# UP with 512 moving columns, the routing's second parts on GpSimd, 16-bit index lookups, and norms spread a unit later in a two-block transformer kernel

## The chip, the cores and the metric

One core of a Trainium2 chip. The metric is the device time of one execution in microseconds (us). Engines: PE (TensorE, matmuls), DVE (VectorE), ACT (ScalarE), POOL (GpSimd), SP (which issues the DMAs of the weights).

## The reference

Two transformer blocks on 256 tokens of 1024 channels in float32, one after the other. The first has an mLSTM beside sliding-window attention, then cross attention to a memory of 256 tokens, then a PEER feed-forward layer. The second has gated linear attention (GLA) beside block attention, an MLP of 4096 and a gated embedding. Each sublayer is led by an RMS norm. The change is in the PEER layer (and in how norms and weights are scheduled):

```python
def peer_ffn(xn, w_pq, sub_keys1, sub_keys2, expert_down, expert_up):   # T = 128 tokens a block
    def block(xb):
        qh = (xb @ w_pq).reshape(T, P_HEADS, 2, P_KEY_DIM)              # 8 heads, 2 halves
        s1 = einsum('thd,nd->thn', qh[:, :, 0], sub_keys1)              # 128 keys each
        s2 = einsum('thd,nd->thn', qh[:, :, 1], sub_keys2)
        v1, i1 = top_k(s1, 16)
        v2, i2 = top_k(s2, 16)
        cand_s = (v1[..., :, None] + v2[..., None, :]).reshape(T, P_HEADS, 256)
        cand_i = (i1[..., :, None] * 128 + i2[..., None, :]).reshape(T, P_HEADS, 256)
        top_s, pos = top_k(cand_s, 16)
        eidx = take_along_axis(cand_i, pos, axis=-1)                    # the lookup
        g = softmax(top_s, axis=-1)
        a = gelu(einsum('thkd,td->thk', expert_down[eidx], xb))
        return einsum('thk,thkd->td', g * a, expert_up[eidx])
```

## The kernel before

*Residual and weights.* The residual `hT` stands with channels in partitions (8 tiles of 128 x 256 tokens). All weights come as one stream of chunks of 128 x 1024 f32 (512 KB), in the order of `ORDER`. `Stream` (from L88) has SP load a chunk into `raw` (4 buffers). `cut_upto` splits it into two parts that the matmuls take: `hi`, a rounded copy (L122, always by ACT here), and `lo` = raw - hi (L123, the second part, by DVE or by GpSimd). Which engine does it stands in `PLAN`: a chunk's name starts a pattern that holds until the next name, and a pattern's letters are A, V, G for ACT, DVE and GpSimd (`AV`: hi on ACT, lo on DVE; from pq2 on GpSimd has two chunks of three, from down52 none, in UP every other one). There are 3 buffers of hi and lo; a chunk is cut when the one two before it is taken. The activations are split too (`XH`, `XL`), and each product is three matmuls: hi by XH, hi by XL, lo by XH.

*Two forms of a product.* `unit_T` (L323 to L325) has the weights as the stationary operand and 256 tokens moving; a chunk is 24 matmuls and gives one tile of 128 outputs. `unit_N` (L362 to L364) has 128 tokens of the activation stationary and 512 columns of weights moving; a chunk is 12 matmuls.

*Order.* All engines' instructions are in the order in which the Python code issues them. `Chains` holds generators, the work beside the stream: after each unit `tick` lets each go on by one step; `yield n` passes n units, to which the table `PAUSES` adds.

*PEER.* After the queries (16 units `pq`) and their scores come 128 units `down`, in which every expert is multiplied with every token (`ev_down`, gelu on ACT). Beside the first 52 units runs `routing()`, on DVE but for the softmax's exp. For each of two blocks of 128 tokens (tb) it does 16 searches of the 16 best of 128 (`top16`, two per unit), 8 searches in 256 candidate sums (L872 builds the sums; one per unit), the softmax (L876 to L880), and two lookups. A lookup turns a candidate's position into the index of a key: L895 compares the position with 0 to 15 (2048 f32 per partition), L898 multiplies by the indices, L899 sums over the 16, and a transpose (L902) brings the result into `eT`. Then `gating()` builds coefficients of all 128 x 128 experts by matmuls of 16-bit one-hot rows (L918 to L922, L941). `UP` follows: for each of 128 chunks, `coef` (L974 by ACT, L975 by DVE) splits a coefficient tile into the `ring`, and `up` (L987 to L989) adds 24 matmuls to four PSUM banks: weights stationary, 256 tokens moving. So UP's sums have channels in partitions, like hT. The last two chunks are taken together; for each pair of output tiles the sums are added to hT (L1013), then scaled and split into XH (L1018) and XL (L1021), while PE multiplies the next pair. At 1121.5 us the second block begins with `bk` (unit_N).

*Norms.* A `norm_chain` (L308) sums squares over channels with a matmul, takes an inverse square root by Newton steps on DVE, makes a diagonal, and `gap` units later `spread` (L305) brings it to all partitions with two matmuls. The cross attention's query norm, FFN's norm and the MLP's and last norms use it; the second block's first norm is written out in `norms` and `along`; the GLA's gate (L1127, L1129) is a chain too.

## Time and profile before

| what | value |
|---|---|
| median of 3 runs | 1644.19 us (1643.83 to 1645.55) |
| the profiled execution | 1648.56 us |
| its span, first to last instruction | 1646.8 us |
| mean granted clock of PE | 0.981 |
| PE / DVE / ACT / POOL busy | 1572.9 / 1207.7 / 798.9 / 392.0 us |
| DMA | 265.52 MB, mean 161 GB/s |

Stages in the profiled execution: the queries' units from 240, the scores from 293, DOWN 301.1 to 752.6 with the routing until 504.9, UP 752.7 to 1121.5, the second block from there. The profile's page gives busy time per engine, then the costliest groups of instructions; other views of the trace show a stretch, an engine's waits with what released them, or single instructions in time. A matmul's duration there is that of its way through the array; how fast PE goes shows in the distance between the starts of two.

### The profile page before, as it was taken

Reading aid. Unit: us, or ns where it says so; the run is one execution under the profiler, and the core shown is the slowest. Engines: PE = TensorE matmul, PEld = TensorE weight load, DVE = VectorE, ACT = ScalarE, POOL = GpSimd, SP = SyncE. Lnnn points to the kernel's source line nnn. Section 1 sums busy time; section 2 is a strip of 40 time slices with the busy share of each in tenths; the row PEclk is TensorE's granted clock in tenths of the full one; section 3 lists DMA queues with packets and bytes.
Section 4 is the critical chain, followed back from the end, with each engine's and each line's share of the span. In section 5 each row is a group of like instructions: output and inputs, shape, how many; then the busy total and the mean of one; then the engine's idle time right before and its main releaser. Section 6 shows DMA issues by size and latency. Waiting matters only on the chain.

```text
span 1646.8 us, 30594 instructions
## 1 busy us (share of the span) xinstructions
PE 1572.9 (96%) x12338; PEld 1515.7 (92%) x12338; DVE 1207.7 (73%) x2073; ACT 798.9 (49%) x1336; POOL 392.0 (24%) x223
## 2 busy tenths in 40 slices
PE   9889989989879999999999999999899999899998
PEld 8788989988879999999999999998698899899998
DVE  6967653788978899976666666668885566777556
ACT  7555443543334555544444444445464643444444
POOL 3210004435530000003444444421030100087000
PEclk9999999999989999999999999999999999999999
DMA  7334444334334444445665555665445345455653
GB/s 263 103 103 156 139 145 154 131 131 162 128 123 158 156 154 154 154 168 178 183 185 184 180 180 184 186 186 166 152 143 164 119 163 179 159 175 190 201 180 128
DMA packets 75726, 265.52 MB, mean 161 GB/s; under 512 B 8368, under 2 KB 11952, under 8 KB 75584
## 3 DMA queue, kind: packets, MB, share of 16 engines
q1 hardware_dynamic: 74848, 262.31, 48.7%
q8 instruction: 96, 1.57, 0.4%
q10 hardware_dynamic: 736, 1.27, 0.2%
q14 instruction: 46, 0.38, 0.1%
HBM read 262.49 MB, written 1.05 MB: 160 GB/s over the span
## 4 chain that ended last, share of the span: by engine, by line
PE 63%; DVE 6%; ACT 1%; issue 1%; POOL 0%; DVEq 0%; POOLq 0%; ACTq 0%
PE mm L323 11%; PE mm L325 11%; PE mm L324 10%; PE at L987 6%; PE at L988 6%; PE at L989 6%; DVE lo L123 2%; PE mm L989 2%; PE mm L988 2%; PE mm L987 2%; PE at L941 2%; PE mm L363 2%; PE mm L362 2%; PE mm L364 2%; ACT hi L122 1%
## 5 line engine op out<-in xcount | busy, mean ns | idle before, releaser
L122 ACT CAST hi<-raw 128x1024 fp32r<-128x1024 f32 (+1 forms) x495 | 515.6, 1044 | 301.0 <-issue 104.9
L123 DVE TENSOR_TENSOR lo<-raw,hi 128x1024 fp32r<-128x1024 f32 (+1 forms) x376 | 469.9, 1252 | 167.1 <-ACT hi L122 164.0
L123 POOL TENSOR_TENSOR lo<-raw,hi 128x1024 fp32r<-128x1024 f32 x119 | 296.2, 2489 | 843.5 <-ACT hi L122 708.4
L325 PE MATMUL mm<-XH,lo 128*128 128x256 f32 x1608 | 464.3, 289 | 32.2 <-DVE lo L123 31.5
L323 PE MATMUL mm<-XH,hi 128*128 128x256 f32 x1608 | 470.9, 293 | 4.8 <-DVE hT L378 4.3
L324 PE MATMUL mm<-XL,hi 128*128 128x256 f32 x1608 | 461.7, 287 | 0.0
L325 PEld LDWEIGHTS mm<-XH,lo 128*128 128x128 f32 x1608 | 315.6, 196 | 35.9 <-DVE lo L123 34.8
L323 PEld LDWEIGHTS mm<-XH,hi 128*128 128x128 f32 x1608 | 315.9, 196 | 6.6 <-issue 5.1
L324 PEld LDWEIGHTS mm<-XL,hi 128*128 128x128 f32 x1608 | 315.9, 196 | 0.2
L975 DVE SCALAR_TENSOR_TENSOR ring<-cb,ring 128x256 fp32r<-128x256 f32 x128 | 173.0, 1353 | 94.1 <-ACT ring L974 94.1
L987 PE MATMUL at<-ring,hi 128*128 128x256 f32 x768 | 217.4, 283 | 1.0 <-DVE cb L961 1.0
L988 PE MATMUL at<-ring,hi 128*128 128x256 f32 x768 | 217.4, 283 | 0.0
L989 PE MATMUL at<-ring,lo 128*128 128x256 f32 x768 | 217.4, 283 | 0.0
L987 PEld LDWEIGHTS at<-ring,hi 128*128 128x128 f32 x768 | 147.4, 192 | 1.2 <-ACT ring L974 1.2
L988 PEld LDWEIGHTS at<-ring,hi 128*128 128x128 f32 x768 | 147.4, 192 | 0.1
L989 PEld LDWEIGHTS at<-ring,lo 128*128 128x128 f32 x768 | 147.5, 192 | 0.0
L958 ACT ACTIVATE cb<-mm 128x256 f32<-128x256 f32 (+32 forms) x117 | 38.2, 326 | 171.7 <-PE mm L325 171.7
L363 PE MATMUL mm<-lo,XH 128*128 128x512 f32 (+1 forms) x208 | 82.0, 394 | 4.8 <-DVE lo L123 4.7
L362 PE MATMUL mm<-hi,XH 128*128 128x512 f32 (+1 forms) x208 | 84.1, 404 | 1.0 <-ACT kn L1336 1.0
L364 PE MATMUL mm<-hi,XL 128*128 128x512 f32 (+1 forms) x208 | 81.6, 392 | 0.8 <-DVE XL L411 0.8
L325 PE MATMUL mm<-MH,lo 128*128 128x256 f32 x256 | 72.5, 283 | 2.0 <-POOL lo L123 1.2
L988 PE MATMUL mm<-ring,hi 128*128 128x256 f32 x256 | 72.5, 283 | 0.0
(460 smaller groups left out, 2932.0 us busy)
## 6 DMA issues: line engine op xcount, KB each, us to landing
raw<-in_wst SPq DMA_DIRECT2D x237, 512.0 KB, 3.3
raw<-in_dwn SPq DMA_DIRECT2D x128, 512.0 KB, 3.3
raw<-in_upw SPq DMA_DIRECT2D x128, 512.0 KB, 4.1
hT<-in_xT SPq DMA_DIRECT2D x4, 256.0 KB, 5.4
memt<-in_memT SPq DMA_DIRECT2D x1, 1024.0 KB, 6.0
out<-hT SPq DMA_DIRECT2D x7, 128.0 KB, 1.7
rowt<-in_rows ACTq DMA_DIRECT2D x1, 640.0 KB, 6.0
raw<-in_wst SPq DMA_DIRECT2D x2, 256.0 KB, 3.9
```

Of the source, the lines that this page charges most:

```text
L122: self.nc.scalar.copy(hi[:, o], raw[:, o])
L123: (self.nc.vector if second == "V" else self.nc.gpsimd).tensor_tensor(lo[:, o], raw[:, o], hi[:, o], op=OP.subtract)
L323: T.matmul(ps, lhsT=wh, rhs=xh, start=start, stop=False)
L324: T.matmul(ps, lhsT=wh, rhs=xl, start=False, stop=False)
L325: T.matmul(ps, lhsT=wl, rhs=xh, start=False, stop=stop)
L362: T.matmul(pss[tb], lhsT=xh, rhs=h, start=kd == 0, stop=False)
L363: T.matmul(pss[tb], lhsT=xh, rhs=l, start=False, stop=False)
L364: T.matmul(pss[tb], lhsT=xl, rhs=h, start=False, stop=kd == 7)
L975: V.scalar_tensor_tensor(lo, cb[:, j], 1.0 / GATE, hi, op0=OP.mult, op1=OP.subtract)
L987: T.matmul(o, lhsT=wh, rhs=ch, start=j == 0 and n % 2 == 0, stop=False)
L988: T.matmul(o, lhsT=wh, rhs=cl, start=False, stop=False)
L989: T.matmul(o, lhsT=wl, rhs=ch, start=False, stop=j == 127 and n % 2 == 1)
```

## The change

Four parts. **UP** becomes the other form: 128 tokens of the coefficients are stationary, 512 columns of weights move, half as many matmuls (12 per chunk). Its sums now have tokens in partitions, so at the end they are copied out of PSUM (one half per token block by ACT, one by DVE, L1041 and L1042), turned by 16 transposes (L1026), added to hT (L1030) and split (L1032, L1034); the second half of the channels follows as a chain after `bk0`. **PLAN**: from xo2 on, GpSimd makes all second parts, but those of down20 to down27 and from down45 on, which are DVE's. **The lookup** works on 16-bit numbers: the indices are copied twice side by side (L896), compare (L898) and product (L902) run over 2048 float16, the sum over 16 is three halving additions (L904) and a last one (L905); a chain step more lies between a lookup and its transpose. **Norms**: the spread comes a unit later (but for the first norm), and so do the second block's first norm and a step of the GLA's gate.

```diff
-          ("along", 1): 2, ("stream", 0): 1, ...
+          ("along", 1): 3, ("stream", 0): 1, ...
-          ("gla", 8): 1, ("gla_out", 2): 1}
+          ("gla", 1): 1, ("gla", 8): 1, ("gla_out", 2): 1}
-PLAN = {"mv0": ("AV",), "pq2": ("AG", "AG", "AV"), "down52": ("AV",), "upw0": ("AV", "AG"), "upw122": ("AV",),
-        "up3": ("AV", "AG"), "up31": ("AV",)}
+PLAN = {"mv0": ("AV",), "xo2": ("AG",), "down20": ("AV",), "down28": ("AG",), "down45": ("AV",),
+        "upw0": ("AV", "AG"), "upw122": ("AV",), "up3": ("AV", "AG"), "up31": ("AV",)}
...
-    def norm_chain(pool, tag, work, nat, dst, total=None, gap=1):
+    def norm_chain(pool, tag, work, nat, dst, total=None, gap=2):
...
-            yield from norm_chain(psA, "at", wk, rx, Rb)
+            yield from norm_chain(psA, "at", wk, rx, Rb, gap=1)
...
-            yield from norm_chain(psA, "at", wk, rm, Rm, total=accm, gap=2)
+            yield from norm_chain(psA, "at", wk, rm, Rm, total=accm, gap=3)
...
-                V.tensor_copy(fi, iu)
...
-                    V.tensor_tensor(cand.rearrange("p h a b -> p (h a) b"),
-                                    pf[:, :, None].to_broadcast([128, 128, 16]),
-                                    iota[:, None, 0:16].to_broadcast([128, 128, 16]), op=OP.is_equal)
-                    V.tensor_tensor(cand, cand, ff[:, :, half, None, :].to_broadcast([128, 8, 16, 16]), op=OP.mult)
-                    V.tensor_reduce(ee, cand.rearrange("p h a b -> p (h a) b"), axis=AX.X, op=OP.add)
-                    yield 4
+                    V.tensor_copy(two, uu[:, :, half].rearrange("p h k -> p k h")[:, :, :, None].to_broadcast(
+                        [128, 16, 8, 2]))
+                    V.tensor_tensor(hit.rearrange("p k (c s) -> p k c s", s=2),
+                                    pf.rearrange("p (c s) -> p c s", s=2)[:, None].to_broadcast([128, 16, 64, 2]),
+                                    iota2[:, 0:16, None, :].to_broadcast([128, 16, 64, 2]), op=OP.is_equal)
+                    h5 = hit.rearrange("p k (h c s) -> p k h c s", h=8, s=2)
+                    V.tensor_tensor(h5, h5, two[:, :, :, None, :].to_broadcast([128, 16, 8, 8, 2]), op=OP.mult)
+                    for n in (8, 4, 2):
+                        V.tensor_tensor(hit[:, 0:n], hit[:, 0:n], hit[:, n:2 * n], op=OP.add)
+                    V.tensor_tensor(ee, hit[:, 0], hit[:, 1], op=OP.add)
+                    yield 5
...
-        sums = [bank(psB, "at") for i in range(3)] + [bank(psB, "mm")]
+        sums = [[bank(psB, "mm") for tb in range(2)] for g in range(2)]
+        nat2 = flat[:, 4096:6144].rearrange("p (a d) -> p a d", a=2)
...
-        def up(j, w, n):
-            o = sums[n // 2][:, (n % 2) * 256:(n % 2) * 256 + 256]
-            wh, wl = (x[:, n * 128:n * 128 + 128] for x in w)
-            ch, cl = coefs[j]
-            T.matmul(o, lhsT=wh, rhs=ch, start=j == 0 and n % 2 == 0, stop=False)
-            T.matmul(o, lhsT=wh, rhs=cl, start=False, stop=False)
-            T.matmul(o, lhsT=wl, rhs=ch, start=False, stop=j == 127 and n % 2 == 1)
+        def up(j, w, tb, g):
+            ch, cl = (c[:, tb * 128:tb * 128 + 128] for c in coefs[j])
+            wh, wl = (x[:, g * 512:g * 512 + 512] for x in w)
+            o = sums[g][tb]
+            T.matmul(o, lhsT=ch, rhs=wh, start=j == 0, stop=False)
+            T.matmul(o, lhsT=ch, rhs=wl, start=False, stop=False)
+            T.matmul(o, lhsT=cl, rhs=wh, start=False, stop=j == 127)
...
-        for i in range(4):
-            for n in (2 * i, 2 * i + 1):
-                for j in range(2):
-                    up(126 + j, last[j], n)
-            k2 = slice(2 * i, 2 * i + 2)
-            V.tensor_tensor(hT[:, k2], sums[i].rearrange("p (a t) -> p a t", a=2), hT[:, k2], op=OP.add)
...
+        def half(g):
+            turned = {}
+            for i in (2 * g, 2 * g + 1):
+                turned[i] = bank(psB, "at")
+                for k in range(2):
+                    for tb in range(2):
+                        o = (2 * i + k) * 128
+                        T.transpose(turned[i][:, k * 256 + tb * 128:k * 256 + tb * 128 + 128], nat2[:, tb, o:o + 128],
+                                    ident)
+            for i in (2 * g, 2 * g + 1):
+                k2 = slice(2 * i, 2 * i + 2)
+                V.tensor_tensor(hT[:, k2], turned[i].rearrange("p (a t) -> p a t", a=2), hT[:, k2], op=OP.add)
+                for n in (2 * i, 2 * i + 1):
+                    A.activation(XH[:, n], hT[:, n], AF.Copy, scale=gfm[:, n:n + 1])
+                for n in (2 * i, 2 * i + 1):
+                    V.scalar_tensor_tensor(XL[:, n], hT[:, n], gfm[:, n:n + 1], XH[:, n], op0=OP.mult,
+                                           op1=OP.subtract)
+
+        for g in range(2):
+            for tb in range(2):
+                for j in range(2):
+                    up(126 + j, last[j], tb, g)
+            A.copy(nat2[:, 0, g * 512:g * 512 + 512], sums[g][0])
+            V.tensor_copy(nat2[:, 1, g * 512:g * 512 + 512], sums[g][1])
+        half(0)
+        ws.cut_upto(ws.taken + 2)
...
+        def second_half():
+            half(1)
...
```

How DVE's instructions stand in three places, before and in the changed kernel (line, operation, what it writes from what it reads, shape; `cb` is the large scratch tile in which the routing's tensors lie).

DVE in the routing, the searches in 256 candidates of one head (L872 builds the sums), before:

```order
L872 TENSOR_TENSOR cb<-cb 128x256
L855 MAX cb<-cb 128x8
L856 MAX_INDEX cb<-cb 128x8
L857 MATCH_REPLACE cb<-cb 128x256
L858 MAX cb<-cb 128x8
L859 MAX_INDEX cb<-cb 128x8
L123 TENSOR_TENSOR lo<-raw,hi 128x1024
L872 TENSOR_TENSOR cb<-cb 128x256
```

and now (the search's lines are one higher, L856 to L860):

```order
L872 TENSOR_TENSOR cb<-cb 128x256
L856 MAX cb<-cb 128x8
L857 MAX_INDEX cb<-cb 128x8
L858 MATCH_REPLACE cb<-cb 128x256
L859 MAX cb<-cb 128x8
L860 MAX_INDEX cb<-cb 128x8
L872 TENSOR_TENSOR cb<-cb 128x256
```

The second parts (L123) that stood after every third search are gone from DVE here.

DVE in the first block of tokens, from the softmax's end to the first lookup's transpose, before:

```order
L123 TENSOR_TENSOR lo<-raw,hi 128x1024
L886 TENSOR_SCALAR gT<-at 128x128
L887 SCALAR_TENSOR_TENSOR gT<-at,gT 128x128
L891 TENSOR_SCALAR cb<-cb 128x128
L894 CAST cb<-cb 128x128
L895 TENSOR_TENSOR cb<-cb,iota 128x2048
L898 TENSOR_TENSOR cb<-cb 128x2048
L899 TENSOR_REDUCE cb<-cb 128x128
L123 TENSOR_TENSOR lo<-raw,hi 128x1024
```

and now, from the position's shift on:

```order
L891 TENSOR_SCALAR cb<-cb 128x128
L894 CAST cb<-cb 128x128
L896 CAST cb<-cb 128x256
L898 TENSOR_TENSOR cb<-cb,iota_93 128x2048
L902 TENSOR_TENSOR cb<-cb 128x2048
L904 TENSOR_TENSOR cb<-cb 128x1024
L904 TENSOR_TENSOR cb<-cb 128x512
L904 TENSOR_TENSOR cb<-cb 128x256
L905 TENSOR_TENSOR cb<-cb 128x128
L123 TENSOR_TENSOR lo<-raw,hi 128x1024 x5
L909 CAST eT<-at 128x128
```

Compare, product and sum (three rows) became seven of smaller or 16-bit tensors, and five second parts instead of one lie between a lookup and its transpose (L903, now L909).

DVE at UP's end and the second block's beginning, before:

```order
L123 TENSOR_TENSOR lo<-raw,hi 128x1024 x2
L1013 TENSOR_TENSOR hT<-at,hT 128x512 x2
L1021 SCALAR_TENSOR_TENSOR XL<-hT,gfm,XH 128x256 x2
L1013 TENSOR_TENSOR hT<-at,hT 128x512
L1021 SCALAR_TENSOR_TENSOR XL<-hT,gfm,XH 128x256 x2
L1013 TENSOR_TENSOR hT<-mm,hT 128x512
L123 TENSOR_TENSOR lo<-raw,hi 128x1024
L1021 SCALAR_TENSOR_TENSOR XL<-hT,gfm,XH 128x256 x4
L123 TENSOR_TENSOR lo<-raw,hi 128x1024 x4
```

and now:

```order
L123 TENSOR_TENSOR lo<-raw,hi 128x1024 x2
L1042 COPY cb<-mm 128x512 x2
L1030 TENSOR_TENSOR hT<-at,hT 128x512
L1034 SCALAR_TENSOR_TENSOR XL<-hT,gfm,XH 128x256 x2
L1030 TENSOR_TENSOR hT<-at,hT 128x512
L1034 SCALAR_TENSOR_TENSOR XL<-hT,gfm,XH 128x256 x2
L123 TENSOR_TENSOR lo<-raw,hi 128x1024 x2
L1030 TENSOR_TENSOR hT<-at,hT 128x512
L1034 SCALAR_TENSOR_TENSOR XL<-hT,gfm,XH 128x256 x2
L1030 TENSOR_TENSOR hT<-at,hT 128x512
L1034 SCALAR_TENSOR_TENSOR XL<-hT,gfm,XH 128x256 x2
L123 TENSOR_TENSOR lo<-raw,hi 128x1024 x3
```

The additions to hT no longer alternate with matmuls of UP: two copies out of PSUM come first, then all of the first half, and the second half comes behind two second parts of the second block.

## Rows read from the trace of the kernel before

**Rows 1.** The page's busy times by engine, with the share of the span and the number of instructions.

```profile
PE 1572.9 (96%) x12338; PEld 1515.7 (92%) x12338; DVE 1207.7 (73%) x2073; ACT 798.9 (49%) x1336; POOL 392.0 (24%) x223
```

**Rows 2.** Busy time by stage: the window and its length in us, then each engine's busy us (instructions), PE's granted clock, the busy share of the DMA engines and GB/s. The windows are the end of xo with the first of pq, the part of DOWN in which the routing runs, UP, and the beginning of the second block.

```profile
212.80:256.00 43.20, 36.96 (x286) 36.37 (x285) 26.22 (x55) 18.88 (x30) 5.51 (x3) 0.91 0.39 129
301.10:505.20 204.10, 172.35 (x1307) 169.31 (x1306) 176.01 (x463) 78.61 (x116) 89.56 (x33) 0.92 0.40 137
752.60:1121.50 368.90, 368.83 (x3072) 368.78 (x3073) 252.90 (x202) 175.76 (x261) 144.18 (x60) 1.00 0.59 183
1121.50:1194.00 72.50, 64.83 (x295) 50.84 (x293) 61.84 (x188) 39.42 (x55) 10.70 (x13) 0.95 0.47 155
```

**Rows 3.** Single matmuls in time on PE: start in us, modelled duration in us, line, operation, tiles. The first is UP's first, the last the second block's first; the two between are 24 matmuls apart.

```profile
752.67 0.35 PE L987 MATMUL at<-ring,hi 128*128 128x256 f32 x1 [1.01 <-DVE cb L961]
899.76 0.28 PE L987 MATMUL at<-ring,hi 128*128 128x256 f32 x1
902.64 0.28 PE L987 MATMUL at<-ring,hi 128*128 128x256 f32 x1
1121.52 0.40 PE L362 MATMUL mm<-hi,XH 128*128 128x512 f32 x1
```

**Rows 4.** PE's waits from 301.1 to 505.2: what waited, for whose write, us in all, times, the longest.

```profile
PE mm L325 <- DVE lo L123: 29.3, 12, 6.6
PE at L902 <- DVE cb L899: 1.7, 1, 1.7
PE mm L325 <- POOL lo L123: 0.7, 1, 0.7
```

**Rows 5.** PE in time, in two streams of 512 moving columns: 12 matmuls lie from the first row to the second, and 9 from the third to the fourth.

```profile
1130.00 0.39 PE L362 MATMUL mm<-hi,XH 128*128 128x512 f32 x1
1132.72 0.39 PE L362 MATMUL mm<-hi,XH 128*128 128x512 f32 x1
150.45 0.39 PE L362 MATMUL mm<-hi,memh 128*128 128x512 f32 x1
152.55 0.40 PE L362 MATMUL mm<-hi,memh 128*128 128x512 f32 x1
```

**Rows 6.** PE in time: the first of 16 transposes of the second block, and the matmul after them.

```profile
1178.12 0.60 PE L1243 MATMUL at<-ident,kn 128*128 128x128 f32 x4
1179.81 0.48 PE L362 MATMUL mm<-hi,XH 128*128 128x512 f32 x1
```

**Rows 7.** Groups of like instructions from 1117 to 1194 (end of UP, beginning of the second block): line, engine, operation, tiles and shapes, count; busy us, mean ns of one; idle us before them and the releaser. L1018 writes XH, L1245 copies from PSUM, L1013 adds from PSUM.

```profile
L1018 ACT ACTIVATE XH<-hT,gfm 128x256 fp32r<-128x256 f32 x8 | 3.6, 498 | 1.9 <-DVE hT L1013 1.9
L1245 ACT COPY qk<-at 128x512 f32<-128x512 f32 x6 | 3.2, 595 | 3.4 <-PE at L1243 3.4
L1013 DVE TENSOR_TENSOR hT<-at,hT 128x512 f32<-128x512 f32 x3 | 2.1, 688 | 0.1
```

**Rows 8.** Groups of like instructions from 301.1 to 505.2, columns as before.

```profile
L123 POOL TENSOR_TENSOR lo<-raw,hi 128x1024 fp32r<-128x1024 f32 x33 | 89.6, 2714 | 108.5 <-ACT hi L122 108.4
L898 DVE TENSOR_TENSOR cb<-cb 128x2048 f32<-128x2048 f32 x4 | 15.4, 3856 | 0.1
L872 DVE TENSOR_TENSOR cb<-cb 128x256 f32<-128x256 f32 x16 | 15.1, 946 | 0.0
L895 DVE TENSOR_TENSOR cb<-cb,iota 128x2048 f32<-128x2048 f32 x4 | 11.3, 2826 | 0.1
L899 DVE TENSOR_REDUCE cb<-cb 128x128 f32<-128x2048 f32 x4 | 9.1, 2286 | 0.1
L918 DVE TENSOR_TENSOR hots<-eT,iota 128x1024 f16<-128x1024 f16 x1 | 0.7, 681 | 0.0
```

**Rows 9.** The same from 212.8 to 256.

```profile
L123 DVE TENSOR_TENSOR lo<-raw,hi 128x1024 fp32r<-128x1024 f32 x9 | 11.0, 1224 | 3.6 <-ACT hi L122 3.6
L123 POOL TENSOR_TENSOR lo<-raw,hi 128x1024 fp32r<-128x1024 f32 x3 | 7.1, 2371 | 125.6 <-ACT hi L122 125.6
L289 DVE SCALAR_TENSOR_TENSOR XL<-hT,colt,XH 128x256 fp32r<-128x256 f32 x8 | 3.9, 484 | 4.6 <-ACT XH L288 4.6
L299 DVE TENSOR_TENSOR acc<-acc,sq 128x256 f32<-128x256 f32 x7 | 2.9, 418 | 0.0
```

**Rows 10.** PE's waits over the whole span, columns as in the waits above.

```profile
PE mm L323 <- DVE hT L378: 4.3, 1, 4.3
PE at L1127 <- DVE gl L1129: 2.4, 2, 1.8
PE at L305 <- DVE dg L318: 2.1, 2, 1.6
PE at L305 <- DVE cb L318: 1.6, 1, 1.6
PE at L305 <- DVE dg L1076: 1.4, 1, 1.4
```

**Rows 11.** GpSimd (POOL) and DVE in time, where both had work.

```profile
335.14 2.39 POOL L123 TENSOR_TENSOR lo<-raw,hi 128x1024 fp32r<-128x1024 f32 x1 [6.50 <-ACT hi L122]
335.64 2.97 DVE L123 TENSOR_TENSOR lo<-raw,hi 128x1024 fp32r<-128x1024 f32 x1
373.44 4.37 POOL L123 TENSOR_TENSOR lo<-raw,hi 128x1024 fp32r<-128x1024 f32 x1 [0.58 <-ACT hi L122]
375.57 4.39 DVE L898 TENSOR_TENSOR cb<-cb 128x2048 f32<-128x2048 f32 x1
```

More of the change, by code (lines that the diff above doesn't have):

```diff
@@ L70 @@
 PAUSES = {("norm0", 1): 1, ("mlstm", 12): 1, ("window", 0): 1, ("window", 3): 2, ("norms", 0): 1, ("norms", 2): 1,
-          ("along", 1): 2, ("stream", 0): 1, ("stream", 1): -3, ("stream", 2): -2, ("stream", 4): 1, ("stream", 5): 1,
+          ("along", 1): 3, ("stream", 0): 1, ("stream", 1): -3, ("stream", 2): -2, ("stream", 4): 1, ("stream", 5): 1,
           ("keys", 0): 1, ("keys", 1): 1, ("keys", 2): 3, ("keys", 3): 1, ("keys", 4): 2, ("queries", 1): 3,
-          ("gla", 8): 1, ("gla_out", 2): 1}
-PLAN = {"mv0": ("AV",), "pq2": ("AG", "AG", "AV"), "down52": ("AV",), "upw0": ("AV", "AG"), "upw122": ("AV",),
-        "up3": ("AV", "AG"), "up31": ("AV",)}
+          ("gla", 1): 1, ("gla", 8): 1, ("gla_out", 2): 1}
+PLAN = {"mv0": ("AV",), "xo2": ("AG",), "down20": ("AV",), "down28": ("AG",), "down45": ("AV",),
+        "upw0": ("AV", "AG"), "upw122": ("AV",), "up3": ("AV", "AG"), "up31": ("AV",)}
 def chunks(s):
@@ L812, in block_kernel @@
         iu = carve([128, 16, 16], U32)
-        fi = carve([128, 16, 16])
         ts = carve([128, 8, 16])
@@ L816, in block_kernel @@
         px = carve([128, 8, 16], U32)
-        pf = carve([128, 128])
+        pf = carve([128, 64]).bitcast(F16)
+        two = carve([128, 128]).bitcast(F16).rearrange("p (k h s) -> p k h s", k=16, s=2)
         ee = carve([128, 128])
@@ L821, in block_kernel @@
         xn = cand.rearrange("p h a b -> p h (a b)")
+        hit = cand.rearrange("p h a b -> p (h a b)")[:, 0:1024].bitcast(F16).rearrange("p (k c) -> p k c", k=16)
         assert base <= 128 * 256, base
@@ L862, in routing @@
             vv = v.rearrange("p (h a) k -> p h a k", a=2)
-            ff = fi.rearrange("p (h a) k -> p h a k", a=2)
+            uu = iu.rearrange("p (h a) k -> p h a k", a=2)
             e3 = ee.rearrange("p (h k) -> p h k", h=8)
@@ L993, in block_kernel @@
             w = ws.take(f"upw{j}")
-            for n in range(8):
-                up(j, w, n)
+            for tb in range(2):
+                for g in range(2):
+                    up(j, w, tb, g)
         last = [ws.take("upw126"), ws.take("upw127", 1)]
@@ L1006, in square @@
             A.activation(sq1[:, k2], hT[:, k2], AF.Square)
-        for i in range(4):
-            for n in (2 * i, 2 * i + 1):
-                for j in range(2):
-                    up(126 + j, last[j], n)
-            k2 = slice(2 * i, 2 * i + 2)
-            V.tensor_tensor(hT[:, k2], sums[i].rearrange("p (a t) -> p a t", a=2), hT[:, k2], op=OP.add)
-            if i == 3:
-                ws.cut_upto(ws.taken + 2)
-                square(2)
-            for n in (2 * i, 2 * i + 1):
-                A.activation(XH[:, n], hT[:, n], AF.Copy, scale=gfm[:, n:n + 1])
-            for n in (2 * i - 2, 2 * i - 1) if i < 3 else (4, 5, 6, 7):
-                if n >= 0:
+        def half(g):
[13 more added lines that the diff above has]
+                for n in (2 * i, 2 * i + 1):
                     V.scalar_tensor_tensor(XL[:, n], hT[:, n], gfm[:, n:n + 1], XH[:, n], op0=OP.mult,
                                            op1=OP.subtract)
-            if i != 2:
-                square(i)
+        for g in range(2):
+            for tb in range(2):
+                for j in range(2):
[4 more added lines that the diff above has]
+        ws.cut_upto(ws.taken + 2)
+        square(0)
+        square(1)
+        def second_half():
+            half(1)
+            yield 1
+            square(2)
+            square(3)
+        ch.start("half", second_half())
         ws.cut_upto(ws.taken + 3)
```

## The prediction

> **What bounds the kernel now.** I read the busy shares first, then busy time and granted clock by stage, then the matmul engine's waits within the stages that the change touches, and last the spacing of single matmuls. PE is busy 1572.9 of 1646.8 us [rows 1], so a gain must either shorten PE's own stream or close one of its few gaps. The stage table says where each is to be had [rows 2]. In UP (752.6 to 1121.5) PE has no gap at all and the clock is 1.00: this stage is its matmul stream, and nothing but fewer or cheaper matmuls shortens it. While the routing runs (301.1 to 505.2) PE is busy 172.35 of 204.1 us at a granted clock of 0.92, and DVE is the fullest of the engines beside it (176.01).
>
> What that stretch loses can be counted. It holds the down units 0 to 52, each 24 matmuls of 256 columns. In the undisturbed UP stream 24 matmuls take 2.88 us (899.76 to 902.64 [rows 3]), so 53 units would take 152.6 us, and 51.5 us are lost. PE's waits make 31.7 of them, 29.3 of it for DVE's second parts (lo), in 12 waits of up to 6.6 us [rows 4]. The clock makes 0.08 x 204.1 = 16.3: the mean lies between the two levels of 1.2 and 2.4 GHz, and PE had stood still in the gaps before it fell. The rest is transposes and small change. So DVE is the bound here, in its lateness and not in its share: a lo stands in DVE's queue behind a block of routing work, and the unit after next needs it.
>
> **The change, part by part.** The sum is made against the profiled execution, 1648.56 us (span 1646.8); the median of the runs is 1644.19, 4.4 lower. A gain in us is taken off both alike.
>
> 1. *UP's matmuls, 256 columns to 512.* 3072 matmuls ran from 752.67 to 1121.52, which is 368.85 us or 120.1 ns each [rows 3]. Afterwards there are 1536 with 512 moving columns. The kernel has two such streams: 12 matmuls in 2.72 us (1130.00 to 1132.72), 226.7 ns each, and 9 in 2.10 us (150.45 to 152.55), 233.3 ns each [rows 5]. The first follows UP in a stretch fed as UP is; I take it. 1536 x 0.2267 = 348.2, a gain of **20.4 us** (10.4 at 233.3). The feeders don't become the bound: DVE was busy 252.90, ACT 175.76 and POOL 144.18 of 368.9 us, DMA 0.59 of its time [rows 2]; at 348 us that is DVE 73% and DMA 63%.
> The Trainium skill ("TensorE: Matmul & The Clock Gate", section "Back-to-back issue gap") puts an isolated warm matmul at columns/2.4 GHz plus 2.5 ns, by which halving their number would save only 1536 x 2.5 ns = 3.8 us. The rows disagree with the size of it: two matmuls of 256 columns take 240 ns and one of 512 takes 226.7, a difference of 13. It is a rival below, by way of the spacing.
>
> 2. *UP's end.* Before, each pair of sums was added to hT while the next pair was multiplied, and PE went into the second block at 1121.52 without a gap [rows 3]. Now the sums lie with tokens in partitions, and 16 transposes come first. Sixteen transposes of the second block run from 1178.12 to 1179.81, 1.7 us [rows 6]. The first half's copies from PSUM (ACT 0.60, DVE 0.69 [rows 7]) lie beside the last 12 matmuls (2.7 us); but after its transposes PE waits for DVE's add (0.69) and ACT's XH (0.50), with DVE's other copy and semaphores about 2.0. Then DVE owes adds, XL and three second parts at once (the last order piece): I put 0.7 for the second chunk's lo, 0.9 for the fifth XH and 1.8 for the fourth chunk's lo, all estimates, from L123's and L1018's lengths in a queue that is already late. With the transposes **+7 us**, between +3 (transposes and the first wait) and +11 (all late parts in series and a fall of the clock).
>
> 3. *Routing without DVE's second parts.* GpSimd takes every chunk but those from down20 to down27 and from down45 on. A second part takes it 2.71 us here and 2.37 in xo and pq, on the mean [rows 8, 9], below a unit's 2.88. DVE's own backlog then holds up nothing that PE wants, except in the lookups. The cost of a lookup on DVE before: 2.83 + 3.86 + 2.29 = 9.0 us for compare, product and sum of 2048 f32 [rows 8]. Now these are 16-bit. The nearest row is the gating's compare of 1024 16-bit values with broadcasts, 0.69 us [rows 8]; so 2048 take 1.4, twice; the additions 0.7, 0.35, 0.2 and 0.2; casts and shifts about 1.5: 5.7 us. A part is cut two units (5.8 us) ahead and needs 1.22 itself [rows 9], so I leave 1.1 us of waiting at each of 4 lookups; 1 for the softmax, which goes through ACT; 2.7 where the parts return to DVE at down45: 8 us. The clock then costs about 5 instead of 16.3, as the waits fall to a quarter of 31.7 but come as often at the few places left. 13 instead of 51.5: **-38 us**. The bounds: -48 if nothing waits; -15 if GpSimd is blocked as in rival A.
>
> 4. *xo and pq.* From xo2 on GpSimd takes these too. The stretch 212.8 to 256 loses 6.2 us of PE [rows 2], 4.3 of it once for hT and 1.6 for the FFN norm's spread [rows 10]. Moving lo of 1.22 off DVE would help the first, but 2.37 on GpSimd plus DVE's XL (0.48) and the sum of squares (0.42 [rows 9]), if they exclude each other, are 3.3 us against PE's 2.88 per unit. I take **0**, from -6 to +6.
>
> 5. *Spreads one unit later.* PE waited 2.1 us in two places at L305 for a norm's diagonal, 1.4 for the second block's first norm and 2.4 for the GLA's gate [rows 10]. A unit of matmuls now stands in front of each. The second 1.4 is used up by the later end of UP, since its chain begins later too; the others go: **-4.5**, from 0 (if the chains' later readers wait in turn) to -9 (with the clock that comes back). The FFN norm's 1.6 is within term 4.
>
> Sum: -20.4 + 7 - 38 + 0 - 4.5 = -55.9. From 1648.56 that is 1592.7, and from the median **1588 us**.
>
> **Rivals.**
> A. *GpSimd becomes the bound in part.* DVE operations with two inputs and GpSimd's hold each other up: a DVE lo begun at 335.64 beside GpSimd's from 335.14 took 2.97 us instead of 1.22, and GpSimd's from 373.44 took 4.37 behind a DVE product of 4.39 [rows 11]; L872's mean of 946 ns is lifted by this too. If this goes on in the lookups, the 16-bit operations don't reach their rate there. For it: 59 chunks in a row or nearly so now lie on GpSimd (six of xo, 16 pq, down0 to 19 and 28 to 44). Against: in the top-16 searches only L872 takes two inputs (one per unit); alone it is as long as L299 (0.42), and 2.37 + 0.42 = 2.79 us is still under 2.88. Price: 4 lookups x 5 us and 0.06 us on each of 59 units give 23.5: 1612. Chance 0.15.
> The Trainium skill ("SBUF — State Buffer", section "Who interferes with whom") says the same pair of ports is an exclusive lock between GpSimd and a DVE operation with two SBUF inputs, which speaks against handing more work to GpSimd. The rows just named agree.
> B. *UP gains less.* 512 columns at 233.3 ns, or a spacing a little higher because each of the 512-column streams shown is short (12 and 9 matmuls): UP gains 0 to 10 instead of 20.4, 1598 to 1608, middle 1603. For it: the second row. Against: the other one is steady at 1.00 clock. Chance 0.13. By the page named in term 1 the gain would be 3.8 and the time 1605.
> C. *All the routing's loss goes*, with the clock: 13 us less, 1575. For it: 2.71 is less than 2.88. Against: the lookups still stand in DVE's queue ahead of eight chunks' parts. Chance 0.08.
> D. *Slower.* Every GpSimd second part between xo2 and down44 is held up in turn, as the one at 373.44. At 4.37 us each of 59 chunks takes 4.37 - 2.88 = 1.49 us longer: 88 us, with 13 at the switches 101. Before, 51.5 + 10.1 (waits and clock of xo and pq) were lost, so 39 are added; with -20.4 + 7 - 4.5 that is +21, 1665 us. It decides when the mean second part is above 2.88 + (61.6 - 13 + 17.9)/59 = 4.0 us. Against: the 33 parts of that stretch, some of them beside DVE's worst operations, average 2.71 [rows 8]. Chance 0.04.
>
> **How the numbers follow.** The forecast has 0.60, A 0.15, B 0.13, C 0.08, D 0.04. The range reaches from C's 1575 a little down, since term 5 may give 9 and term 2 only 3, and up past A with a late end of UP: 1570 to 1618; it leaves out D and about 0.12 of the others' tails. A change of 0.2% (3.3 us) is about what a measurement of this kernel can tell from none. All cases but D lie over 0.2% below: faster 0.94, within 0.2% 0.02, slower 0.04.
>
> **What would show it.** In the profile after: UP's matmuls 226.7 ns apart and the stage 348 us (A and C leave that, B breaks it); GpSimd's second parts averaging 2.4 to 2.7 between xo2 and down44 (A: 2.8 to 3.2; D: above 4.0); PE's waits for lo between the first down unit and the first product of the gating under 10 us instead of 30, with the clock near 0.97; the lookup's product at 1.4 us instead of 3.86; 16 transposes and about 5 us of waits at the beginning of the second block. The forecast is wrong if the routing's stretch still loses over 30 us or UP's spacing is above 232 ns.

## The result, and the profile after

The changed kernel takes 1587.22 us (three runs of 1585.12 to 1587.23) against 1644.01 for the kernel before: a ratio of 0.9649, 95% interval 0.963 to 0.9668. That is 57.7 us less (54.6 to 60.8). A fourth run of it took 3015.01 us and is left out as slow; nothing on record shows why. The forecast was 1588 (1570 to 1618).

The page after, busy times first (beside [rows 1]):

```profile
PE 1535.7 (97%) x10818; PEld 1420.5 (90%) x10818; DVE 1163.8 (73%) x2070; ACT 799.6 (50%) x1338; POOL 417.4 (26%) x238
```

PE's busy share rose by a point only, because its own stream became shorter too: 37 us less busy, 24 us less idle. Busy time and clock by stage, windows as in [rows 2] but moved to the same places of the program:

```profile
209.40:246.50 37.10, 35.84 (x300) 35.46 (x298) 22.39 (x30) 18.73 (x30) 28.72 (x12) 1.00 0.50 149
291.60:469.50 177.90, 170.57 (x1401) 169.36 (x1399) 141.37 (x475) 83.72 (x123) 84.21 (x35) 0.99 0.54 169
705.80:1054.00 348.20, 348.12 (x1536) 288.47 (x1537) 250.25 (x196) 174.62 (x256) 144.05 (x60) 1.00 0.61 193
1054.00:1128.00 74.00, 65.23 (x305) 51.16 (x304) 62.29 (x187) 37.66 (x56) 10.89 (x13) 0.97 0.46 150
```

The clock is 1.00 in xo and pq (0.91 before) and 0.99 in the routing's stretch (0.92). The first of these is not the same in every execution: the wait of 2.8 us at the FFN norm's spread was followed by 3.4 us at half clock in four later kernels that run the same instructions up to it (e5a, e5b, e9 and e11, below), and by none here and in e12. UP is 348.2 us long, without a gap. The second block's beginning is not better off: 65.23 us busy of 74.0 (64.83 of 72.5 before). By the first and last matmuls of each stage, in us:

| stage | before | after | difference |
|---|---|---|---|
| up to the first down unit | 301.1 | 291.6 | -9.5 |
| DOWN | 451.6 | 414.3 | -37.3 |
| UP | 368.9 | 348.3 | -20.6 |
| second block | 520.5 | 526.2 | +5.7 |

This sums to 61.6, four more than the medians say: the profiled execution before was 4.4 above its median. It spent 10.2 us at half clock before 100 us, where nothing relevant differs, and the one after 3.4; that is 3.4 us of the first row, as half clock costs at most half its length. In the second block it is the other way round, 6.8 us before and 10.2 after, some 1.7 of the 5.7.

PE's waits in the routing's stretch, beside [rows 4] (29.3, 1.7 and 0.7 before):

```profile
PE mm L325 <- DVE lo L123: 7.3, 6, 2.9
```

Over the whole span, beside [rows 10]:

```profile
PE mm L325 <- DVE lo L123: 10.9, 13, 2.9
PE mm L363 <- DVE lo L123: 9.0, 11, 2.1
PE at L305 <- DVE cb L318: 2.8, 1, 2.8
```

The hT wait of 4.3 is 0.6 (not among these rows), the GLA's gate went from 2.4 to 1.2, but the FFN norm's spread waits longer than before (2.8 for 1.6), and the unit_N products (L363) wait 9.0 us for a second part instead of 5.3.

Groups of like instructions in the routing's stretch, beside [rows 8]:

```profile
L123 POOL TENSOR_TENSOR lo<-raw,hi 128x1024 fp32r<-128x1024 f32 x35 | 84.2, 2406 | 50.7 <-ACT hi L122 50.7
L872 DVE TENSOR_TENSOR cb<-cb 128x256 f32<-128x256 f32 x16 | 9.8, 610 | 0.0
L902 DVE TENSOR_TENSOR cb<-cb 128x2048 f16<-128x2048 f16 x4 | 4.9, 1224 | 0.1
L898 DVE TENSOR_TENSOR cb<-cb,iota 128x2048 f16<-128x2048 f16 x4 | 4.9, 1219 | 0.0
```

GpSimd's second parts are 2.41 us long on the mean and none is longer than 2.46; L872 is at 610 ns (946). The lookup's compare and product take 1.22 us each for 2048 16-bit values. UP's matmuls, beside [rows 3] and [rows 5]:

```profile
850.16 0.39 PE L996 MATMUL mm<-hi,ring 128*128 128x512 f32 x1
...
852.20 0.39 PE L996 MATMUL mm<-hi,ring 128*128 128x512 f32 x1
```

Nine matmuls lie from the first row to the second, 2.04 us, 226.7 ns each.

### The profile page after: what moved, and what is told of

It reads as the page before. It is cut to its first block, busy times and chain, and to the rows that moved or that the text cites. A ratio compares the mean times of both kernels' runs of the same rounds, so it can differ in the third digit from the quotient of the medians.

```text
span 1585.4 us, 27640 instructions
## 1 busy us (share of the span) xinstructions
PE 1535.7 (97%) x10818; PEld 1420.5 (90%) x10818; DVE 1163.8 (73%) x2070; ACT 799.6 (50%) x1338; POOL 417.4 (26%) x238
## 3 DMA queue, kind: packets, MB, share of 16 engines
HBM read 262.49 MB, written 1.05 MB: 166 GB/s over the span
## 4 chain that ended last, share of the span: by engine, by line
PE 73%; DVE 18%; ACT 5%; issue 3%; DMA 0%; POOL 0%; SPq 0%; DVEq 0%; ACTq 0%; POOLq 0%
PE mm L323 13%; PE mm L325 13%; PE mm L324 13%; PE mm L998 7%; PE mm L996 7%; PE mm L997 7%; DVE lo L123 5%; ACT hi L122 3%; PE mm L364 2%; PE mm L363 2%; PE mm L362 2%; PE at L947 2%; DVE cb L860 1%; DVE cb L857 1%; DVE scr L1263 1%
## 5 line engine op out<-in xcount | busy, mean ns | idle before, releaser
L123 DVE TENSOR_TENSOR lo<-raw,hi 128x1024 fp32r<-128x1024 f32 (+1 forms) x361 | 443.5, 1233 | 150.5 <-ACT hi L122 145.3
L123 POOL TENSOR_TENSOR lo<-raw,hi 128x1024 fp32r<-128x1024 f32 x134 | 322.5, 2407 | 755.6 <-ACT hi L122 618.4
L325 PE MATMUL mm<-XH,lo 128*128 128x256 f32 x1608 | 457.9, 285 | 9.2 <-DVE lo L123 9.2
L325 PEld LDWEIGHTS mm<-XH,lo 128*128 128x128 f32 x1608 | 309.9, 193 | 11.2 <-DVE lo L123 11.0
L323 PEld LDWEIGHTS mm<-XH,hi 128*128 128x128 f32 x1608 | 309.8, 193 | 2.9 <-issue 1.5
L324 PEld LDWEIGHTS mm<-XL,hi 128*128 128x128 f32 x1608 | 310.1, 193 | 0.2
L996 PE MATMUL mm<-hi,ring 128*128 128x512 f32 x512 | 199.5, 390 | 1.0 <-DVE cb L967 1.0
L998 PE MATMUL mm<-hi,ring 128*128 128x512 f32 x512 | 199.5, 390 | 0.0
L997 PE MATMUL mm<-lo,ring 128*128 128x512 f32 x512 | 199.4, 390 | 0.0
L996 PEld LDWEIGHTS mm<-hi,ring 128*128 128x128 f32 x512 | 96.2, 188 | 21.0 <-ACT ring L980 1.2
L997 PEld LDWEIGHTS mm<-lo,ring 128*128 128x128 f32 x512 | 96.2, 188 | 20.0
L998 PEld LDWEIGHTS mm<-hi,ring 128*128 128x128 f32 x512 | 96.2, 188 | 19.8
L363 PE MATMUL mm<-lo,XH 128*128 128x512 f32 (+1 forms) x208 | 82.2, 395 | 8.4 <-DVE lo L123 8.4
L325 PE MATMUL mm<-MH,lo 128*128 128x256 f32 x256 | 72.8, 284 | 2.7 <-DVE lo L123 1.5
L323 PE MATMUL mm<-u,hi 128*128 128x256 f32 x256 | 71.8, 281 | 0.0
```

The costliest lines, as they stand in the source:

```text
L123: (self.nc.vector if second == "V" else self.nc.gpsimd).tensor_tensor(lo[:, o], raw[:, o], hi[:, o], op=OP.subtract)
L323: T.matmul(ps, lhsT=wh, rhs=xh, start=start, stop=False)
L324: T.matmul(ps, lhsT=wh, rhs=xl, start=False, stop=False)
L325: T.matmul(ps, lhsT=wl, rhs=xh, start=False, stop=stop)
L363: T.matmul(pss[tb], lhsT=xh, rhs=l, start=False, stop=False)
L996: T.matmul(o, lhsT=ch, rhs=wh, start=j == 0, stop=False)
```

## The experiments

All were timed beside the kernel before, in three sets; the median of the kernel before was 1647.2, 1644.2 and 1647.0 us in them (e1 to e4; e5a to e8; e9 to e12), and the changed kernel had been timed before all three. So two kernels of different sets are better compared by their ratios than by their medians. "Against before" is (ratio - 1) x 1644 us; the interval in brackets is the ratio's, at 95%.

| kernel | median us | ratio (interval) | against before, us |
|---|---|---|---|
| the change | 1587.22 | 0.9649 (0.9630 to 0.9668) | -57.7 |
| e1_up: UP's form alone | 1630.49 | 0.9906 (0.9890 to 0.9921) | -15.5 |
| e2_plan: table of second parts alone | 1618.11 | 0.9836 (0.9819 to 0.9853) | -27.0 |
| e3_lookup: 16-bit lookup alone | 1639.59 | 0.9954 (0.9936 to 0.9972) | -7.6 |
| e4_norms: later spreads alone | 1646.01 | 1.0005 (0.9994 to 1.0016) | +0.8 |
| e6_plan_lookup: table and lookup | 1605.60 | 0.9760 (0.9742 to 0.9779) | -39.5 |
| e8_no_norms: the change without the later spreads | 1593.85 | 0.9690 (0.9671 to 0.9709) | -51.0 |
| e12_no_up: the change without UP's form | 1600.56 | 0.9725 (0.9712 to 0.9738) | -45.2 |
| e5a_ag_tb0: GpSimd through the first lookups | 1592.14 | 0.9685 (0.9666 to 0.9705) | -51.8 |
| e5b_ag_all: GpSimd through all lookups | 1589.49 | 0.9665 (0.9646 to 0.9684) | -55.1 |
| e9_hybrid: GpSimd through the second lookups | 1584.88 | 0.9626 (0.9613 to 0.9639) | -61.5 |
| e10_hybrid_pq: the same, DVE's parts beside the FFN norm | 1583.21 | 0.9615 (0.9601 to 0.9629) | -63.3 |
| e11_wait: GpSimd through all, transposes later | 1583.16 | 0.9618 (0.9600 to 0.9635) | -62.8 |

### The four parts, each alone

The edits are the four parts of the diff above, one at a time on the kernel before.

e1_up:

> UP's new form alone, all else as before. Theory (the terms of the sum): the stream gains 20.5 us (226.7 ns a matmul) and the end costs about 7, so 1630 to 1632. Rival (the later norms are what makes the second block's beginning late): the end costs under 3 here, 1626 or less. Rival (the stream gains only what the others let it): spacing above 230 ns, 1636 or more.

Measured 15.5 us less (13.0 to 18.1). By the profile UP took 348.3 us, 20.6 less than before, and the second block 525.5 instead of 520.5: the end costs 5.0. This profile has 3.4 us less at half clock there than the one before; with half of that added the end costs some 6.7 (an estimate). So the theory's size holds, and the end's price is there without the later spreads. Where it arises stands in the trace of the changed kernel, PE and then DVE at UP's end (beside [rows 6, 7]):

```profile
1053.94 0.39 PE L998 MATMUL mm<-hi,ring 128*128 128x512 f32 x1
1054.17 1.03 PE L1026 MATMUL at<-ident,cb 128*128 128x128 f32 x8
1056.25 0.50 PE L362 MATMUL mm<-hi,XH 128*128 128x512 f32 x1 [1.05 <-ACT XH L1032]
```

```profile
1054.37 0.69 DVE L1042 COPY cb<-mm 128x512 f32<-128x512 f32 x1 [2.03 <-PE mm L998]
1054.97 0.68 DVE L1030 TENSOR_TENSOR hT<-at,hT 128x512 f32<-128x512 f32 x1
...
1059.64 1.22 DVE L123 TENSOR_TENSOR lo<-raw,hi 128x1024 fp32r<-128x1024 f32 x1 [0.46 <-ACT hi L122]
```

The eight transposes of the first half start right behind UP's last matmul and take 1.03 us; PE then waits 1.05 us for XH, which waits for DVE's addition (L1030), which had stood behind DVE's copy (L1042). The second parts come after all of that, behind ACT's hi of the same chunk.

e2_plan:

> Only the table of second parts (GpSimd from xo2 on). Theory (DVE's lateness in the searches is the loss): the waits of 1.84 us at every third search go (seven of them, 13 us, and about as much of half clock), xo and pq gain about 6, the lookups' waits stay or grow: 1612 to 1622. Rival (the shared port: GpSimd's parts hold up the f32 lookups and are held up): GpSimd's mean second part above 2.8 us and the routing's stretch gains under 10 us, 1630 or more.

Measured 27.0 us less (24.2 to 29.8); DOWN is 25.3 us shorter in the profile. All seven waits of 1.84 us at the searches are gone. What is left in the routing's stretch are four waits at lookups (and one short one):

```profile
PE mm L325 <- DVE lo L123: 15.8, 5, 5.6
```

```profile
L123 POOL TENSOR_TENSOR lo<-raw,hi 128x1024 fp32r<-128x1024 f32 x35 | 84.1, 2404 | 58.1 <-ACT hi L122 58.1
L123 DVE TENSOR_TENSOR lo<-raw,hi 128x1024 fp32r<-128x1024 f32 x18 | 21.3, 1220 | 15.6 <-ACT hi L122 15.5
L895 DVE TENSOR_TENSOR cb<-cb,iota 128x2048 f32<-128x2048 f32 x4 | 9.2, 2292 | 0.1
L898 DVE TENSOR_TENSOR cb<-cb 128x2048 f32<-128x2048 f32 x4 | 9.2, 2292 | 0.1
```

GpSimd's mean is 2.40 us here, not above 2.8: the rival is out. Without GpSimd parts beside them the f32 compare and product take 2.29 us instead of 2.83 and 3.86 [rows 8]; the lookup is still 7 us, and a second part behind it is late by up to 5.6.

The table hardly takes second parts away from DVE in this stretch. In the kernel before DVE made 21 of them there beside GpSimd's 33 [rows 8]; now it is 18 beside 35, and DVE is busy 84% of the stretch after 86%. What changed is which chunks DVE has: none among the searches.

```profile
L123 DVE TENSOR_TENSOR lo<-raw,hi 128x1024 fp32r<-128x1024 f32 x21 | 32.8, 1571 | 11.7 <-ACT hi L122 11.7
```

The mean of 1571 ns in the kernel before (1220 now) tells that queue order was not all of it. In each of the seven waits DVE's second part had begun beside one of GpSimd's and ended 1.08 to 1.09 us after that one's end; six of the seven were stretched from 1.22 to between 1.94 and 2.97 us, 7.3 us in all of the 12.8 that PE waited. The pair at 335 in [rows 11] is one of them, and PE waited for it:

```profile
338.67 0.39 PE L325 MATMUL mm<-XH,lo 128*128 128x256 f32 x1 [1.84 <-DVE lo L123]
```

So the two engines' holding each other up, which the rival expected of the new table, was at work in the old one. The table ended both causes in the searches at once; no run takes them apart.

e3_lookup:

> Only the 16-bit lookup with its step more. Theory: it takes away the lookups' own waits (4.67, 1.67, 6.62 and 2.1 us before) but none of the searches': 1630 to 1636. Rival (without the new table DVE is as late as before whatever a lookup costs): within 4 us of before.

Measured 7.6 us less (4.6 to 10.5), between the theory and its rival. The trace tells why it is little. The first of the four waits that the theory gives to lookups, 4.67 us at 352, stands before the first lookup begins (at 370): DVE had built a head's sums beside a GpSimd part, in 2.41 us instead of 0.41, and the second part behind them was late. In the kernel before:

```profile
345.87 2.38 POOL L123 TENSOR_TENSOR lo<-raw,hi 128x1024 fp32r<-128x1024 f32 x1 [5.02 <-ACT hi L122]
346.13 2.41 DVE L872 TENSOR_TENSOR cb<-cb 128x256 f32<-128x256 f32 x1
```

Here this wait is 4.68, and another of 4.68 has come at 460. And with the old table GpSimd's parts run beside the lookup too, and some of the 16-bit operations wait for them:

```profile
L902 DVE TENSOR_TENSOR cb<-cb 128x2048 f16<-128x2048 f16 x4 | 7.0, 1748 | 0.1
```

On the mean of four the product is 1.75 us here (one took 3.32) and 1.22 in the changed kernel, the addition of 1024 is 1.23 instead of 0.69. The searches' waits of 1.8 to 2.4 us and most of the half clock stay.

e4_norms:

> Only the spreads a unit later. Theory: the waits at the spreads go, about 4 us with the clock, 1638 to 1641. Rival (the chains' readers wait in turn): 1643 or more.

Measured no difference (+0.8 us, -1.0 to 2.6). The theory falls for this part alone. PE's wait for a second part between 236 and 260 us in this kernel, then what DVE and GpSimd did:

```profile
PE mm L325 <- DVE lo L123: 4.8, 1, 4.8
```

```profile
247.34 2.48 DVE L284 SCALAR_TENSOR_TENSOR rn<-nww,rn 128x1 f32<-128x1 f32 x2
...
250.45 2.40 DVE L284 SCALAR_TENSOR_TENSOR rn<-nww,rn 128x1 f32<-128x1 f32 x2
252.77 0.47 DVE L318 TENSOR_SCALAR cb<-ident,rn 128x128 f32<-128x128 f32 x2
253.16 1.21 DVE L123 TENSOR_TENSOR lo<-raw,hi 128x1024 fp32r<-128x1024 f32 x1
```

```profile
247.41 2.40 POOL L123 TENSOR_TENSOR lo<-raw,hi 128x1024 fp32r<-128x1024 f32 x1 [4.51 <-ACT hi L122]
250.50 2.34 POOL L123 TENSOR_TENSOR lo<-raw,hi 128x1024 fp32r<-128x1024 f32 x1 [0.69 <-ACT hi L122]
```

The wait for the FFN norm's spread (1.6) is gone from its place, but a matmul of the unit that now comes first needs a second part that DVE has behind the Newton steps, two of which GpSimd's parts hold for 2.4 us each. PE waits 4.8 us there instead. In this profile the first down unit begins 0.9 us later than before, though 1.7 us less went to half clock before 100 us; the second block is 3.6 us shorter, 1.7 of it by 3.4 us less at half clock. The two nearly cancel.

### The parts together

e6_plan_lookup:

> The new table of second parts and the 16-bit lookup together, the rest as before. If their gains only add up (27 and 8 us, measured alone), 1610. Theory (they help each other: with the new table DVE serves the lookups' own second parts alone and no GpSimd part lies beside the 16-bit operations, so the 15.5 us that the table alone still lost at four lookups, and the half clock behind them, shrink to about 7): 1599 to 1604.

Measured 39.5 us less (36.3 to 42.4), where the two alone make 34.6, each with an interval of about 3. The median of 1605.6 lies between the two forecasts, outside the theory's 1599 to 1604, and the time alone does not decide. The profile is on the theory's side: the waits for DVE's second parts in this stretch are 7.4 us (15.8 with the table alone, 27.0 with the lookup alone), and DOWN is 38.7 us shorter than before, where the two alone make 25.3 and 8.3, 33.6. By the times alone the 5 us more are not settled.

e8_no_norms:

> The changed kernel with all spreads at their old places. If the later spreads are worth what they are alone (nothing), 1587, as the changed kernel. Theory (alone they lost at the FFN's norm what they won elsewhere, because there a DVE second part came to stand behind the norm; with GpSimd's parts that loss is gone): 5 to 9 us slower than the changed kernel, 1592 to 1596.

Measured 1593.85, 6.6 us above the changed kernel, and the two intervals lie apart: that is what the later spreads are worth inside the change. In its profile the FFN norm's spread waits 3.5 us at 248, with 6.8 us at half clock around it; in the changed kernel 2.8, and no half clock, but 3.4 in four other kernels after the same wait. From the first query unit to DOWN it is 3.3 us longer than there, and the second block 2.4 (528.6 against 526.2).

e12_no_up:

> The changed kernel with UP in its old form. If UP's form is worth the same beside the other parts as alone (15.5 us), 1602.7. Theory (inside the change its end costs more, since PE's new waits at the second block's beginning fall where the clock then drops): it is worth about 12, 1598 to 1600.

Measured 45.2 us less than before, so UP's form is worth 12.5 us inside the change, against 15.5 alone; with intervals of 2 to 3 us each the difference between the two is not settled. The second block is 516.8 us without and 526.2 with the new form, 9.4 more against 5.0 alone. But the half clock in the profiled executions makes this difference: it is 10.2 us with the form and 3.4 without it here, 3.4 with and 6.8 without it alone. With half of each taken off, the end costs some 6.0 inside the change and 6.7 alone (estimates). Nor do the falls come in every execution: e5a and e5b, with the same second block, have 3.4 and 6.8 us of them, and it takes 523.2 and 525.1 us. So it is not shown that the end costs more inside the change.

### The lookups and GpSimd

The edit of the first two is in the table alone:

```diff
-"xo2": ("AG",), "down20": ("AV",), "down28": ("AG",), "down45": ("AV",),
+"xo2": ("AG",), "down45": ("AV",),      (e5a_ag_tb0)
+"xo2": ("AG",), "down57": ("AV",),      (e5b_ag_all)
```

> The changed kernel with GpSimd making the second parts through the first token block's lookups too (no return to DVE for down20 to 27). Theory (held up by each other, as where a 16-bit product took 1.75 us beside GpSimd and 1.22 without): GpSimd's parts there become longer than a unit's 2.88 us and PE waits for them, 1 to 4 us slower than the changed kernel. Rival (PE's waits at lookups come from the DVE queue alone, and GpSimd catches up): the 1.5 us wait at the first lookup goes, 1 to 3 us faster.

> As the kernel with GpSimd through the first token block's lookups, and through the second's as well: DVE's second parts return only at down57. Theory (held up by each other): 2 to 8 us slower than the changed kernel. Rival (queue alone): the waits of 1.5, 1.5, 0.7 and 2.9 us at the lookups and at down45 and half of their clock go, 4 to 8 us faster.

Measured 1592.14 (1591.21 to 1595.25) and 1589.49 (1588.81 to 1591.54), 4.9 and 2.3 us slower than the changed kernel by the medians; all runs of both lie above all of its, though the intervals of the ratios overlap. The direction is the theory's, its reason is not. In the first, PE waits for the lookup itself and not for a second part; DVE and GpSimd at that place:

```profile
PE at L908 <- DVE cb L905: 5.3, 1, 5.3
```

```profile
353.10 2.50 DVE L896 CAST cb<-cb 128x256 f16<-128x256 uint32 x1
355.52 1.21 DVE L898 TENSOR_TENSOR cb<-cb,iota 128x2048 f16<-128x2048 f16 x1
356.76 3.32 DVE L902 TENSOR_TENSOR cb<-cb 128x2048 f16<-128x2048 f16 x1
360.12 7.61 DVE L904 TENSOR_TENSOR cb<-cb 128x1024 f16<-128x1024 f16 x3
```

```profile
348.33 7.11 POOL L123 TENSOR_TENSOR lo<-raw,hi 128x1024 fp32r<-128x1024 f32 x3 [0.23 <-ACT hi L122]
355.71 11.86 POOL L123 TENSOR_TENSOR lo<-raw,hi 128x1024 fp32r<-128x1024 f32 x4 [0.27 <-ACT hi L122]
```

GpSimd's four parts run back to back (11.86 us, 2.97 each), and between two of them DVE gets one operation. A lookup that takes 4.9 us alone (348.12 to 353.03 in the changed kernel) takes 19 (349.08 to 368.05). It isn't ready when PE comes to its transpose, five units later in PE's order. In the second kernel the same happens to the first token block (5.3 us), but the second block's loss is smaller than the changed kernel's with its return to DVE at down45.

That gave three kernels more:

```diff
+"down20": ("AV",), "down28": ("AG",), "down57": ("AV",),                    (e9_hybrid)
+"pq2": ("AV",), "pq5": ("AG",), and as e9_hybrid                            (e10_hybrid_pq)
+"xo2": ("AG",), "down63": ("AV",), and yield 7 if tb == 0 else 6            (e11_wait)
```

> The changed kernel with GpSimd making the second parts through the second token block's lookups, not the first's (DVE's return at down57). From the two kernels before, that differ in this alone: 2 to 3 us faster than the changed kernel, 1584 to 1586. Rival (it depends on what came before it, PE being later there by the first lookup's 5 us): within 1 us of the changed kernel.

> The same with DVE making the second parts of pq2 to pq4, so that no GpSimd part runs beside the FFN norm's Newton steps. Theory (three GpSimd parts stretch that chain from 1.6 to about 8 us, and PE waits 2.8 us at its spread): that wait goes, 2.5 to 4 us faster than the kernel without this edit, 1581 to 1583. Rival (DVE's parts in front of the chain cost as much): no difference.

> GpSimd through both lookups, and the transposes after the lookups 2 units later for the first token block and 1 for the second (DVE's return at down63). Theory (PE's 5.3 and 2.1 us there are its transposes that stand in its order before the stretched lookup is done, not GpSimd's parts being late): these waits go and with them their half clock, 1580 to 1584. Rival (GpSimd's parts are late too, or the gating, begun six units later, ends after the last down unit): 1588 or more.

e9_hybrid: 1584.88, 2.3 below the changed kernel as expected from the pair before (3.8 by the ratios), but its runs (1583.43 to 1587.70) lie across those of the changed kernel and the intervals overlap, so a gain is not shown. e10_hybrid_pq: 1583.21, its runs 1580.33 to 1584.61 all below the changed kernel's lowest; 1.7 below e9_hybrid where 2.5 to 4 were expected, again with runs that overlap. That the wait goes is plain. GpSimd's parts and the FFN norm's chain on DVE in the changed kernel, then the chain in this one:

```profile
240.02 7.09 POOL L123 TENSOR_TENSOR lo<-raw,hi 128x1024 fp32r<-128x1024 f32 x3 [2.05 <-PE at L314]
```

```profile
240.03 0.16 DVE L263 TENSOR_SCALAR nwm<-at 128x2 f32<-128x2 f32 x1 [4.33 <-PE at L314]
240.23 2.23 DVE L270 TENSOR_SCALAR nwi<-nwm 128x2 int32<-128x2 int32 x1
...
242.49 2.32 DVE L272 TENSOR_SCALAR rn<-nwi 128x2 int32<-128x2 int32 x1
...
248.28 0.48 DVE L318 TENSOR_SCALAR cb<-ident,rn 128x128 f32<-128x128 f32 x2
```

```profile
240.22 0.16 DVE L263 TENSOR_SCALAR nwm<-at 128x2 f32<-128x2 f32 x1 [3.20 <-PE at L314]
240.41 0.17 DVE L270 TENSOR_SCALAR nwi<-nwm 128x2 int32<-128x2 int32 x1
...
242.19 0.47 DVE L318 TENSOR_SCALAR cb<-ident,rn 128x128 f32<-128x128 f32 x2
```

From L263 to L318 it is 8.7 us beside three GpSimd parts and 2.4 without; PE's wait of 2.8 at the spread is gone, with 0.5 for a second part in its place. e11_wait: 1583.16 (1580.61 to 1587.04), inside the theory's range. Its waits at the lookups' transposes are 1.7 us in all instead of 7.4, and 1.7 for GpSimd's own parts remain, so a little of the rival holds too. e10_hybrid_pq and e11_wait are the fastest here, some 4 to 6 us (0.3%) below the change by medians and by ratios; e11's interval overlaps the change's, e10's just does not. Both edits together were not tried.

## Why the prediction was right

*UP's stream* (-20.4): right, -20.6. The spacing is 226.7 ns, the row taken and not the 233.3 that rival B leant on. By the Trainium skill's formula for an isolated matmul ("TensorE: Matmul & The Clock Gate", section "Back-to-back issue gap") it would have been an estimated 3.8 us. This trace disagrees: two matmuls of 256 columns (240 ns) cost 13 ns more than one of 512.

*UP's end* (+7): 5.0 alone and 9.4 inside the change by the second block's length, 6.7 and 6.0 with the half clock taken out, within its bounds of 3 and 11. Eight transposes stand at the front and not sixteen, and the first wait was put at 2.0 after them and is 1.05; the late second parts follow as said.

*Routing* (-38): DOWN is 37.3 shorter. The working had two slips that met. The stretch holds 54 units, not 53 (432 of L325's matmuls, 8 a unit), so 48.6 us were lost before, and waits and clock (31.7 and 16.3) make nearly all of it. After, 58 units lose 10.9 where 13 were forecast: waits 7.3 for 8, clock 1.8 for 5. The clock was the mis-sized term: before there were seven falls with the twelve waits for DVE's second parts, 34.1 us at half clock, and now one of 3.4 us with six waits. The lookup's 5.7 us came out at 4.9. The mechanism was half told. The prediction puts DVE's lateness down to its queue and keeps the two engines' holding each other up for rival A; in the kernel before that was already part of the lateness (7.3 of the 12.8 us at the searches, and the sums before the wait of 4.67), so the table had both to end, and what each was worth stays open.

*xo and pq* (0, from -6 to +6): this step failed in size. From 212 us to the first down unit the changed kernel gained 6.9 us in its profile, just outside the bounds, and 5.4 in that of e5a, where the clock fell after the spread's wait. The sum "2.37 + 0.48 + 0.42, if they exclude each other, are 3.3" did not come true: L289 is held (1108 ns on the mean instead of 484), yet it and part of L299 fit between two of GpSimd's parts, and the units of xo follow each other every 2.85 us, as before. The hT wait shrank from 4.3 to 0.6 and the half clock behind it went.

*Spreads* (-4.5): right as a part of this change (6.6), wrong as a step by itself. The prediction costed it as if a wait that moves were a wait that goes. Alone it is +0.8: at the FFN's norm it let a later second part take the wait over. With the new table that part is GpSimd's, which is why it pays inside the change; a kernel with the table and the later spreads alone was not run.

*Rivals.* A (GpSimd holds up the lookups) did not come about because the change takes GpSimd out of the lookups' neighbourhood; where an experiment put it back, the mechanism was there and cost 2 to 5 us, against the 23.5 that A was priced at, and no loss shows where the transposes come later (e11). C is out, since 10.9 us are still lost; D needed second parts of 4.0 us, and they take 2.41.

So the total is nearer than its terms, and by luck: some 7 us won in xo and pq, for which nothing was put down, make up for 3 more lost in the second block and 1 less won in DOWN.

## What to carry to other kernels

Find out what a late result stands behind and what it runs beside: PE's 48 us in the routing were lost to the order of DVE's queue and to GpSimd parts that held DVE's operations up. Giving the urgent chunks to an engine twice as slow with an empty queue was worth 27 us, though beside the routing that engine makes 35 second parts instead of 33; making the work in front of them cheaper was worth 8. A wait that goes can take a fall of the clock with it, so price both, and look at several executions: the same wait had a fall behind it in some and none in others. A wait that is only moved is worth nothing until the next thing that PE needs has been named. Changes that share a queue need not add: by the profiles DOWN won 5 us more by table and lookup together than apart, and the later spreads were worth 7 us inside the change and none alone.

## What the runs showed of the hardware

GpSimd holds up DVE operations with one SBUF input too, which the prediction had left out: a tensor_scalar of 128 x 2 took 2.23 us beside a GpSimd part (0.17 without), a cast of 128 x 256 2.50 us (0.29 without). The Trainium skill ("SBUF — State Buffer", section "Who interferes with whom") counts casts and tensor_scalar among the operations that can contend with GpSimd when their operands meet its conditions, and the trace agrees. The tensor_scalar that reads PSUM (L263, 0.16 us beside a part begun at the same time), the max searches (a MAX of 256 values 0.43 us, beside a part and without) and the lookup's f32 sum over 16 (L899 of the kernel before, 2.29 us both ways) ran at their own speed beside it. With both queues full (e5a) the two engines took turns, one operation each, so short DVE operations paid the most: three additions that take 1.48 us alone took 7.61.
